# A planner's lock rule for the first layer, and the last squares of a norm summed by TensorE

## The chip, the cores and the metric

The kernel runs on one core of a Trainium2 chip, in one launch. The metric is the time of the whole program on the device in microseconds (us), less is better. The engines are named as the profile names them: PE is TensorE's matmuls and PEld its weight loads, DVE is VectorE, ACT is ScalarE, POOL is GpSimd, and SP is the queue from which most transfers are issued. L536 is line 536 of the kernel.

## The reference

One step of a decoder trunk of two layers, width 1024, over 1024 prompt tokens and 8 x 4 sample tokens, all in float32: 1056 columns in the kernel, which keeps tokens along the free axis.

```python
def _rmsnorm(x, gain):
    xf = x.astype(jnp.float32)
    y = xf * lax.rsqrt(jnp.mean(xf * xf, axis=-1, keepdims=True) + EPS)
    return (y * gain.astype(jnp.float32)).astype(x.dtype)

# _trunk: layer 0, layer 1, final norm
x = x + lru_branch(_rmsnorm(x, g0) @ w_in) @ w_out      # convolution, gates, linear recurrence, SiLU gate
x = x + hgrn_branch(_rmsnorm(x, g1) @ w_in) @ w_out     # gated linear attention with state, SiLU gate
return _rmsnorm(x, final_gain), states
```

The rest of the reference (the convolution, both recurrences, their states) is the same in both kernels and is left out here.

## The kernel before

**Products.** Every product is made of three float32r matmuls per 128 rows of the inner dimension (`mm3`, L245 to L247): the operands are split in a high and a low part, and high x high, high x low and low x high are added up in a bank of PSUM. The 1056 columns of the first layer are worked in three chunks of 352. A weight's high part is a copy on ACT (L387 and others), its low part a subtraction (L332) on DVE or POOL.

**The planner.** Nothing is issued in the order in which it is written. [...] Steps of PE with `main=True` keep their order among themselves; the others are free. `plan` is a list scheduler over the engines, `back` turns a finished plan into new keys, `run` repeats this eight times and takes the best, and for the first layer `search` then tries 3000 random changes of the keys in the first 60 us of the plan. The steps are issued in the order of the best plan, so one changed estimate can move many steps. Each engine serves its queue in order. The lock enters `plan` in two places: a POOL step with `both` sets `held` to its end, and a DVE step with `both` that would start before `held` is taken to wait for it.

```python
            if both and e == "DVE" and held > t0:
                us = max(us, held - t0 + us - 0.13)
            ...
            if both and e == "POOL":
                held = end
```

**The start of the first layer.** Eight blocks of x are loaded for each chunk, and six weights for the first six products (gates and convolution inputs of three tiles). For the first chunk, the unscaled x times the gain is split and multiplied at once; the scale 1/rms of the columns is put on when a product leaves PSUM. So the first chunk's products run ahead of its norm and are held in the four banks `mm`. The norm goes so (`squares`, `norm`): ACT and POOL square the blocks (L439, L437), DVE adds them up (L442), PE sums over the partitions with a column of ones (L281), DVE scales the sums (L454), POOL raises them to -0.5 (L456), DVE spreads them on a diagonal (L457 for 256 columns, L460 for 96), PE makes of it a row for all partitions (L462), and for the first chunk ACT copies that out (L884). DVE then reads the products, times the scale (`evac`: L536 for a gate, L489 for a convolution input). For the second and third chunk the scaled x is split before it is multiplied: L467 scales, ACT's L468 makes the high part, L332 the low part. PE fills the time before its operands are there with 48 small matmuls of ones (L738).

**The end.** The last two heads of the second layer's output product are worked as a loop over three ranges of columns, `OUT` = 424, 376 and 256, and in each over eight rows of 128 features. A row is six matmuls, DVE adds the residual (L1841), ACT squares the result (L1843), and POOL adds the square to the range's accumulator `acc` (L1852). A range's norm is made while the next range runs: at its row `RM` = 3 `summed` puts one matmul for each 128 columns on PE (`norm_sum`, L281) and `roots` makes the scales (L1784 on DVE, L1787 on POOL, then the diagonal L1788 and, for a rest under 128 columns, L1792); at row `SM` = 6 `spread` (L1798) makes the row of scales on PE, and `finish` scales the eight rows (DVE L1818, POOL L1816) and sends them out. Sums and spread are `main` steps. In the last range PE sums each square of rows 4 to 7 itself.

Of the kernel before, what the change touches and what calls it, by code (L numbers as in the profile page):

```python
# [19 lines left out]
ALU = mybir.AluOpType  # L20
# [10 lines left out]
SPOTS, SPOTS0 = (6, 9, 0, 2), (2, 5, -1, -1)  # L31
LAST = "12b675b43", "12b67b453", "12b675b43", "1b267543"
K2 = 8 - K1
RM, SM = 3, 6
OUT = ((0, 424), (424, 376), (800, 256))

D = 1024
SEQ = 1024
# [6 lines left out]
KD = D // 128  # L45
ML = WL // 128
H = 8
EPS = 1e-6
# [3 lines left out]
class Flow:  # L52
# [5 lines left out]
    TURNS = 8  # L58
    ends = []

    def __init__(self, until=None, side=1.2):


        self.until = until
        self.side = side
        self.ops = []
        self.writer = {}
        self.readers = {}
        self.main = None
# [32 lines left out]
    def plan(self, key, stop=None):  # L102

        n = len(self.ops)
        left = [len(o[3]) for o in self.ops]
        ready = [0.0] * n
        wait = {e: [] for e in self.ENGINES}
        free = dict.fromkeys(self.ENGINES, 0.0)
        dma = held = 0.0
        for i in range(n):  # L110
            if not left[i]:
                wait[self.ops[i][0]].append(i)
        starts, ends, took, order = [0.0] * n, [0.0] * n, [0.0] * n, []
        for _ in range(n):
            t0, e = min((max(free[e], min(ready[i] for i in q)), e) for e, q in wait.items() if q)
            q = wait[e]
            i = min((j for j in q if ready[j] <= t0), key=lambda j: (key[j], j))
            q.remove(i)
            order.append(i)
            _, us, _, _, _, kb, _, both = self.ops[i]  # L120
            if both and e == "DVE" and held > t0:
                us = max(us, held - t0 + us - 0.13)
            starts[i] = t0
            free[e] = end = t0 + us
            if both and e == "POOL":
# [88 lines left out]
def tile_trunk(ctx: ExitStack, tc: tile.TileContext, xT, prm, hc, w0, wg, wo0, w1, wo1, s_in,  # L214
               yT, h_out, c_out, sp_out, ss_out):
    nc = tc.nc
    V, S, G, T, Q = nc.vector, nc.scalar, nc.gpsimd, nc.tensor, nc.sync
# [57 lines left out]
    def spans(n):  # L275
        return [(a, min(128, n - a)) for a in range(0, n, 128)]

    def norm_sum(sums, acc, n, start, stop):

        for s, (a, u) in zip(sums, spans(n)):  # L280
            T.matmul(s[:u], acc[:, a:a + u], ones[:, :1], start=start, stop=stop)  # L281
# [18 lines left out]
    with ExitStack() as l0:  # L300
        pl = l0.enter_context(tc.tile_pool(name="l0", bufs=1, reuse_waits="tile"))
        fl = Flow("PE")
# [21 lines left out]
        def dve(n, emit, r, w, prio=5, both=False):  # L324
            fl.add("DVE", 0.13 + 0.0011 * n, emit, r, w, prio, both=both)
# [42 lines left out]
        mm, hg = banks("mm", 4), banks("hg", 4)  # L368
# [567 lines left out]

    with ExitStack() as l1:
        p1 = l1.enter_context(tc.tile_pool(name="l1", bufs=1, reuse_waits="tile"))
        fl = Flow(side=0.4)
        banks8 = [next(mm) for _ in range(4)] + [next(hg) for _ in range(4)]  # L940
        mm, side, hg = cycle(banks8[:NMM]), cycle(banks8[NMM:4]), cycle(banks8[4:])
        chains = banks8[:2], banks8[2:4]
# [830 lines left out]
        accs, sqs, dgs, sb = cycle(spare[:2]), cycle(spare[2:5]), cycle(spare[5:7]), spare[7]  # L1773
        nr2 = cycle([(fixed(f"nr2{i}", [128, 4], F32, p1), ("nr2", i)) for i in range(2)])

        def roots(n, sums, ready):

            r, rk = next(nr2)
            dg, dk = next(dgs)
            f, u = n // 128, n % 128  # L1780
            dve(4, lambda: V.memset(r, 1.0), (), (rk,), 0)
            srcs = [(slice(i, i + 1), s[:w]) for i, (s, (_, w)) in enumerate(zip(sums, spans(n)))]
            for q, src in srcs:
                dve(4, lambda q=q, src=src: V.tensor_scalar(r[:src.shape[0], q], src, 1.0 / D, EPS, op0=ALU.mult, op1=ALU.add),  # L1784
                    ready, (rk,), 0)
            w = len(srcs)
            fl.add("POOL", 0.85, lambda: G.tensor_tensor(r[:, :w], r[:, :w], mhalf[:, :w], op=ALU.pow), (rk,), (rk,), 0)  # L1787
            dve(128 * f, lambda: V.tensor_tensor(dg[:, :128 * f].rearrange("p (i n) -> p i n", i=f),  # L1788
                                                 ident[:, None, :].to_broadcast([128, f, 128]),
                                                 r[:, :f, None].to_broadcast([128, f, 128]), op=ALU.mult), (rk,), (dk,), 0)  # L1790
            if u:
                dve(u, lambda: V.tensor_scalar(dg[:, 128 * f:n], ident[:, :u], r[:, f:f + 1], None, op0=ALU.mult), (rk,), (dk,), 0)  # L1792
            return dg[:, :n], dk

        def spread(n, dg, dk, main):

            bc, bk = next(hg)
            fl.add("PE", 0.002 * n, lambda: T.matmul(bc[:, :n], ones, dg, start=True, stop=True), (dk,), (bk,), 0, main=main)  # L1798
            return bc[:, :n], bk

        def summed(acc, ak, n):
            s, sk = next(hg)
            sums = [s[:, i:i + 1] for i in range(4)]
            fl.add("PE", 0.7, lambda: norm_sum(sums, acc, n, True, True), (ak,), (sk,), 0, main=True)
            return roots(n, sums, (sk,))

        def finish(a, n, bc, bk):
            q = slice(a, a + n)
            own = KD - 3 if a else KD
            if a:  # L1810
                act(n, lambda: S.copy(sb[0][:, :n], bc), (bk,), (sb[1],), 0)
            for k in (*range(own, KD), *range(own)):
                x, xk = x2[k][:, q], ykeys(Y2 + k, a, n)
                if k >= own:
                    act(n, lambda x=x, k=k: S.activation(x, x, AF.Copy, scale=pc("gf", k)), xk, xk, 1)
                    pool(n, lambda x=x: G.tensor_tensor(x, x, sb[0][:, :n], op=ALU.mult), (sb[1], *xk), xk, 1)  # L1816
                else:
                    dve(n, lambda x=x, k=k: V.scalar_tensor_tensor(x, x, pc("gf", k), bc, op0=ALU.mult, op1=ALU.mult), (bk, *xk), xk, 1)  # L1818
                dma(yT[k][:, q], x, xk, (), 1, n / 2, S if k % 2 else Q)

        for a, n in OUT:
            q = slice(a, a + n)
            final = a + n == TOK
            cs = [c for c in range(NCH) if c * CH < a + n and (c + 1) * CH > a]
            acc, ak = next(accs)
            for m in range(KD):
                if a and m == RM:
                    dg = summed(*prev[:2], prev[3])
                if a and m == SM:
                    finish(*prev[2:], *spread(prev[3], *dg, True))  # L1830
# [12 lines left out]
                act(n, lambda sq=sq, x=x, n=n: S.activation(sq[:, :n], x, AF.Square), xk, (sk,), 1)  # L1843
                if final and m >= 4:
                    if m == 4:
                        sums = [(next(hg)) for _ in spans(n)]
                        sumk = [k for _, k in sums]
                        sums = [s[:, :1] for s, _ in sums]
                        fl.add("PE", 0.3, lambda acc=acc, n=n, sums=sums: norm_sum(sums, acc, n, True, False), (ak,), sumk, 0)
                    fl.add("PE", 0.3, lambda sq=sq, n=n, m=m, sums=sums: norm_sum(sums, sq, n, False, m == KD - 1), (sk, *sumk), sumk, 0)  # L1850
                elif m:
                    pool(n, lambda acc=acc, sq=sq, n=n: G.tensor_tensor(acc[:, :n], acc[:, :n], sq[:, :n], op=ALU.add), (sk, ak), (ak,), 1)  # L1852
            prev = acc, ak, a, n
# [76 lines left out]
```

## Time and profile before

| what | us |
|---|---|
| median of three runs | 1077.92 (1074.05 to 1078.39) |
| profiled execution | 1074.69 |
| its span, first to last instruction | 1072.9 |
| PE busy | 1046.7 (98%) |
| DVE busy | 783.4 (73%) |
| ACT busy | 675.9 (63%) |
| POOL busy | 510.3 (48%) |
| mean granted clock of TensorE | 0.991 |

The first layer runs to about 520 us, the second from there, and the loop of the final norm from 1031.7 us. A row of the timeline gives start, duration, engine, line, operation, the tiles written and read, their shapes and how many instructions are merged; what stands in brackets is how long the engine was idle before it and for whom it waited. A row of the waits gives who waited for whom, the sum, the number of times, and the longest.

### The profile page before, as it was taken

How to read it: one execution, taken by the hardware profiler on the slowest of the kernel's cores; microseconds unless marked ns; L12 is line 12 of the kernel's file. 1: busy time of each engine (PE TensorE's matmuls, PEld its weight loads, DVE VectorE, ACT ScalarE, POOL GpSimd, SP SyncE). 2: the span in 40 equal slices, each digit the busy share in tenths (PEclk: the TensorE clock that was granted, in tenths of full speed). 3: DMA queues.
4: the chain of work that ended last, by engine and by line, in shares of the span. 5: the costliest groups of instructions: out<-in, count | busy, mean ns of one | idle time of the engine just before them, and what ended most of it. 6: DMA issues, size and time to landing. Idle time of an engine off the chain costs nothing.

```text
span 1072.9 us, 25911 instructions
## 1 busy us (share of the span) xinstructions
PE 1046.7 (98%) x10092; PEld 1018.4 (95%) x10092; DVE 783.4 (73%) x1536; ACT 675.9 (63%) x1526; POOL 510.3 (48%) x532
## 2 busy tenths in 40 slices
PE   9899999999999999999988999999999999999996
PEld 9899999999999999999988999999999989989995
DVE  7899997689798689256678565756557576899646
ACT  6559665966765776233377585858676755765443
POOL 3326443354535355644544555545455453434465
PEclk9899999999999999999999999999999999999998
DMA  8202122123662586444595565656576662734544
GB/s 283 75 15 58 36 64 61 50 64 93 200 201 68 155 260 198 143 155 167 178 226 123 115 163 109 166 103 163 113 177 143 143 156 66 247 109 118 118 96 162
DMA packets 90331, 143.24 MB, mean 134 GB/s; under 512 B 11104, under 2 KB 55904, under 8 KB 90208
## 3 DMA queue, kind: packets, MB, share of 16 engines
q1 hardware_dynamic: 74656, 112.46, 33.5%
q0 software_dynamic: 13248, 26.35, 14.7%
q10 hardware_dynamic: 2304, 2.77, 0.8%
q8 instruction: 79, 1.29, 0.5%
q14 instruction: 44, 0.36, 0.1%
HBM read 81.60 MB, written 33.05 MB: 107 GB/s over the span
## 4 chain that ended last, share of the span: by engine, by line
PE 86%; DVE 8%; DMA 3%; ACT 1%; issue 1%; POOL 0%; ACTq 0%; POOLq 0%; DVEq 0%; SPq 0%
PE mm L245 24%; PE mm L247 23%; PE mm L246 23%; PE hg L1060 2%; PE hg L1277 1%; PE hg L576 1%; PE hg L1169 1%; PE hg L1279 1%; PE hg L1223 1%; PE hg L245 1%; PE hg L247 1%; PE hg L246 1%; DVE t L332 1%; DMA wraw<-in_w_dram 1%; DMA a<-xn 1%; DVE sg L1042 1%
## 5 line engine op out<-in xcount | busy, mean ns | idle before, releaser
L245 PE MATMUL mm<-xh,whi 128*128 128x352 f32 (+1 forms) x1147 | 355.1, 310 | 5.1 <-ACT os L1247 2.8
L246 PE MATMUL mm<-xl,whi 128*128 128x352 f32 (+1 forms) x1147 | 349.9, 305 | 0.2 <-DVE xl L877 0.2
L247 PE MATMUL mm<-xh,wlo 128*128 128x352 f32 (+1 forms) x1147 | 350.0, 305 | 0.0
L245 PEld LDWEIGHTS mm<-xh,whi 128*128 128x128 f32 x1147 | 216.3, 189 | 8.4 <-ACT os L1247 3.0
L246 PEld LDWEIGHTS mm<-xl,whi 128*128 128x128 f32 x1147 | 216.7, 189 | 2.3 <-DVE xl L877 0.4
L247 PEld LDWEIGHTS mm<-xh,wlo 128*128 128x128 f32 x1147 | 216.5, 189 | 0.0
L332 POOL TENSOR_TENSOR wlo<-wraw,whi 128x512 fp32r<-128x512 f32 (+1 forms) x66 | 94.8, 1444 | 88.1 <-ACT whi L387 71.2
L247 PE MATMUL mm<-t,wlo 128*128 128x264 f32 x408 | 115.9, 284 | 2.9 <-DMA wlo<-wraw 2.8
L245 PE MATMUL mm<-t,whi 128*128 128x264 f32 x408 | 118.1, 289 | 0.0
L246 PE MATMUL mm<-t,whi 128*128 128x264 f32 x408 | 115.8, 284 | 0.0
L508 DVE SCALAR_TENSOR_TENSOR k<-xb,prm_sb,k 128x352 f32<-128x352 f32 (+2 forms) x144 | 88.6, 628 | 13.0 <-ACT k L505 9.9
L247 PEld LDWEIGHTS mm<-t,wlo 128*128 128x128 f32 x408 | 76.6, 188 | 3.3 <-DMA wlo<-wraw 3.3
L245 PEld LDWEIGHTS mm<-t,whi 128*128 128x128 f32 x408 | 76.9, 188 | 0.3
L246 PEld LDWEIGHTS mm<-t,whi 128*128 128x128 f32 x408 | 76.9, 189 | 0.1
L591 POOL TENSOR_TENSOR k<-X 128x352 f32<-128x352 f32 x36 | 45.2, 1262 | 55.5 <-DVE R L592 42.8
L1539 DVE TENSOR_TENSOR k<-mm,k 128x264 f32<-128x264 f32 x72 | 30.6, 429 | 53.9 <-PE mm L247 51.5
L319 POOL DMA_DIRECT2D wlo<-wraw x51 | 44.6, 886 | 52.6 <-ACT wlo L318 32.5
L245 PE MATMUL mm<-yh,whi 128*128 128x352 f32 x153 | 49.9, 326 | 0.0
L246 PE MATMUL mm<-yl,whi 128*128 128x352 f32 x153 | 49.4, 323 | 0.0
L247 PE MATMUL mm<-yh,wlo 128*128 128x352 f32 x153 | 49.4, 323 | 0.0
L319 POOL DMA_DIRECT2D wlo<-R x30 | 28.0, 935 | 40.7 <-ACT wlo L318 38.2
L387 ACT CAST whi<-wraw 128x512 fp32r<-128x512 f32 (+1 forms) x63 | 36.1, 591 | 16.8 <-DMA wraw<-in_w_dram 7.2
(423 smaller groups left out, 2723.2 us busy)
## 6 DMA issues: line engine op xcount, KB each, us to landing
wraw<-in_w_dram SPq DMA_DIRECT2D x88, 256.0 KB, 3.2
wlo<-wraw POOLq DMA_DIRECT2D x51, 256.0 KB, 4.1
wlo<-R POOLq DMA_DIRECT2D x30, 256.0 KB, 4.2
wraw<-in_wo_dram SPq DMA_DIRECT2D x37, 192.0 KB, 2.7
ysum<-sg SPq DMA_DIRECT2D x9, 528.0 KB, 4.2
si<-in_s_in_dram SPq DMA_DIRECT2D x8, 512.0 KB, 4.2
R<-in_w_dram SPq DMA_DIRECT2D x16, 256.0 KB, 3.7
out_ss_out_dram<-si SPq DMA_DIRECT2D x8, 512.0 KB, 2.7
```

Source lines behind the costliest of these rows:

```text
L245: T.matmul(out, wh, xh, start=first, stop=False, skip_group_check=chained)
L246: T.matmul(out, wh, xl, start=False, stop=False, skip_group_check=chained)
L247: T.matmul(out, wl, xh, start=False, stop=last, skip_group_check=chained)
L319: fl.add("POOL", 0.93, lambda: G.dma_start(dst.bitcast(F32), src, accum_op=ALU.add), (*r, *w), w, prio, n / 2)
L332: emit = lambda: e.tensor_tensor(b, x, a.bitcast(F32), op=ALU.subtract)
L387: act(m, lambda hi=hi, raw=raw, m=m: S.copy(hi[:, :m], raw[:, :m]), rk, (hk,), prio)
L508: dve(u, lambda src=src, dst=dst, sh=sh, k=k: V.scalar_tensor_tensor(dst, sh(src, k), pc("cw", 12 * k + m), dst, op0=ALU.mult, op1=ALU.add ...
L576: fl.add("PE", 0.62, lambda ps=ps, i=i, c=c: T.matmul(ps[:96, :CH], gs[:, i, :], ST[:96, chunk(c)], start=True, stop=True), (("gs",), *((" ...
L591: pool(CH, lambda x=x, a=a, b=b: G.tensor_tensor(x, a.bitcast(F32), b.bitcast(F32), op=ALU.add), (ak, bk), (xk,), 3)
L1042: dve(n // 2, lambda sv=sv, dv=dv, s=s, f=f: V.tensor_tensor(dv[:, :, s, :], sv[:, :, s, :], f, op=ALU.mult), (*sk, *gk), dk if i == o els ...
L1060: T.matmul(ps[32 * j:32 * j + 32, n * w:n * w + w], B[:, o:o + 32], q(slice(o, o + 32)), start=True, stop=True, tile_position=(0, 32 * j))
L1539: dve(QT, lambda: V.tensor_tensor(o[0], z[0], u[0], op=ALU.add), (z[1], u[1]), (o[1],), 0)
```

## The change

There are two parts.

The planner gets a switch `issues`. [...] It is on for the first layer, whose POOL steps without the mark are the power steps of the norms and the iotas of the masks; the second layer keeps the old rule.

In the final norm, for the first two ranges, POOL adds up the squares of rows 0 to 5 only. PE sums three things into three sets of four columns of one PSUM bank: the accumulator, row 6's square and row 7's square (`PS` = 6). `roots` gets `groups` = 3 and lets DVE reduce the three sets (new lines 1788 and 1790: one `tensor_reduce` for the full blocks of 128 columns, one for a rest, then one scaling). These sums are no longer `main` steps, so the planner places them. The ranges become 416, 384 and 256.

```diff
-OUT = ((0, 424), (424, 376), (800, 256))
+RM, SM, FM, PS = 3, 6, 3, 6
+OUT = ((0, 416), (416, 384), (800, 256))
...
-    def __init__(self, until=None, side=1.2):
+    def __init__(self, until=None, side=1.2, issues=True):
...
-            if both and e == "POOL":
+            if e == "POOL" and (both or self.issues):
                 held = end
...
-        fl = Flow(side=0.4)
+        fl = Flow(side=0.4, issues=False)
...
-        def roots(n, sums, ready):
+        def roots(n, sums, ready, groups=1):
...
+            if groups > 1:
+                view = sums.rearrange("p (g i) -> p i g", i=4)
+                for t in ([128, 0, f],) + (([u, f, f + 1],) if u else ()):
+                    dve(4, lambda t=t: V.tensor_reduce(r[:t[0], t[1]:t[2]], view[:t[0], t[1]:t[2]], op=ALU.add, axis=mybir.AxisListType.X),
+                        ready, (rk,), 0)
+                dve(4, lambda: V.tensor_scalar(r[:, :w], r[:, :w], 1.0 / D, EPS, op0=ALU.mult, op1=ALU.add), (rk,), (rk,), 0)
...
-        def summed(acc, ak, n):
-            s, sk = next(hg)
-            sums = [s[:, i:i + 1] for i in range(4)]
-            fl.add("PE", 0.7, lambda: norm_sum(sums, acc, n, True, True), (ak,), (sk,), 0, main=True)
-            return roots(n, sums, (sk,))
...
                 if a and m == RM:
-                    dg = summed(*prev[:2], prev[3])
+                    dg = roots(prev[1], prev[2], prev[3], KD - PS + 1)
...
+                elif m >= PS and not final:
+                    if m == PS:
+                        s_, sk_ = next(hg)
+                        fl.add("PE", 0.5, lambda s_=s_, acc=acc, n=n: norm_sum([s_[:, i:i + 1] for i in range(4)], acc, n, True, True), (ak,), (sk_,), 0)
+                    o = 4 * (m - PS + 1)
+                    fl.add("PE", 0.5, lambda s_=s_, sq=sq, n=n, o=o: norm_sum([s_[:, o + i:o + i + 1] for i in range(4)], sq, n, True, True), (sk,), (sk_,), 0)
                 elif m:
                     pool(n, lambda acc=acc, sq=sq, n=n: G.tensor_tensor(acc[:, :n], acc[:, :n], sq[:, :n], op=ALU.add), (sk, ak), (ak,), 1)
```

In the second layer the queues stay as they were up to the final norm. In the first layer every queue is rearranged, most in the first 60 us. The lines of the changed kernel are numbered one higher there (L443 is the old L442), and up to line 1776.

The first place is PE's queue in the fourth product of the start (its operands are `xh`, `xl`, `yh` and `yl`), at the spread of the first chunk's norm. Before:

```order
L247 MATMUL mm<-xh,yl_153 128x352
L245 MATMUL mm<-xh,yh_150 128x352
L246 MATMUL mm<-xl,yh_150 128x352
L247 MATMUL mm<-xh,yl_153 128x352
L462 MATMUL hg<-k,ones 128x352
```

Now, at the same spread:

```order
L246 MATMUL mm<-xh,yh_150 128x352
L247 MATMUL mm<-xl,yh_150 128x352
L248 MATMUL mm<-xh,yl_153 128x352
L282 MATMUL hg<-ones,R 128x1 x2
L282 MATMUL hg<-ones,R 96x1
L463 MATMUL hg<-k,ones 128x352
```

Before, the spread stands behind the 15th matmul of the product and the sums of the second chunk's norm behind the 3rd; now both stand together behind the 6th.

The second place is DVE's queue from the end of the first chunk's diagonal to the first read of a product (`R` and `xo` are the accumulator and the squares of the second and third chunk, `nr` the scales, `smalls` small constants of the layer, `mm` the products). Before:

```order
L460 TENSOR_SCALAR k<-ident,nr_130 128x96
L442 TENSOR_TENSOR R<-R,xo_135 128x352
L442 TENSOR_TENSOR R<-R,xo_136 128x352
L454 TENSOR_SCALAR nr_131<-hg 128x2
L454 TENSOR_SCALAR nr_131<-hg 96x1
L442 TENSOR_TENSOR R<-R,xo_137 128x352
L442 TENSOR_TENSOR R<-R,xo_135 128x352
L750 TENSOR_TENSOR smalls<-smalls 128x12
L750 TENSOR_SCALAR smalls<-smalls 128x12
L442 TENSOR_TENSOR R<-R,xo_136 128x352
L442 TENSOR_TENSOR R<-R,xo_137 128x352
L536 TENSOR_TENSOR sg<-mm,R 128x352
```

Now:

```order
L461 TENSOR_SCALAR k<-ident,nr_130 128x96
L443 TENSOR_TENSOR R<-R,xo_137 128x352
L443 TENSOR_TENSOR R<-R,xo_135 128x352
L443 TENSOR_TENSOR R<-R,xo_136 128x352
L751 TENSOR_SCALAR smalls<-smalls 128x12
L751 TENSOR_TENSOR smalls<-smalls 128x12
L455 TENSOR_SCALAR nr_131<-hg 128x2
L455 TENSOR_SCALAR nr_131<-hg 96x1
L443 TENSOR_TENSOR R<-R,xo_137 128x352
L443 TENSOR_TENSOR R<-R,xo_135 128x352
L450 MEMSET nr_130 128x4
L537 TENSOR_TENSOR sg<-mm,R 128x352 x3
```

Five additions stand there instead of six, and three products are read one behind the other, the third bank first. Ahead of these rows, from the first instruction on, DVE's queue holds 14 such additions where it held 15, and seven small steps on `smalls` with 12 elements besides the reciprocal where it held ten. Two additions of the third chunk now come some 30 instructions later.

The third place is PE's queue in the final norm, at the sums of the first range inside the second (`t` holds weights; `R`, `sg` and `a` hold the accumulator and the squares). Before:

```order
L247 MATMUL mm<-xh,t_5231 128x376
L281 MATMUL hg<-ones,R 128x1 x3
L281 MATMUL hg<-ones,R 40x1
L245 MATMUL mm<-xh,t_5232 128x376
L246 MATMUL mm<-xl,t_5232 128x376
```

Now:

```order
L248 MATMUL mm<-xh,t_5230 128x384
L282 MATMUL hg<-ones,R 128x1 x3
L282 MATMUL hg<-ones,R 32x1
L282 MATMUL hg<-ones,sg 128x1 x3
L282 MATMUL hg<-ones,sg 32x1
L282 MATMUL hg<-ones,a 128x1 x3
L282 MATMUL hg<-ones,a 32x1
L246 MATMUL mm<-xh,t_5231 128x384
```

Twelve sums stand where four stood, and one row of features earlier (behind row 1 of the second range instead of row 2). For the second range it is nine instead of three, again one row earlier. The spreads stay ahead of row 6.

More of the change, by code (lines that the diff above doesn't have):

```diff
@@ L33 @@
 K2 = 8 - K1
-RM, SM = 3, 6
-OUT = ((0, 424), (424, 376), (800, 256))
+RM, SM, FM, PS = 3, 6, 3, 6
+OUT = ((0, 416), (416, 384), (800, 256))
 D = 1024
@@ L59 @@
     ends = []
-    def __init__(self, until=None, side=1.2):
+    def __init__(self, until=None, side=1.2, issues=True):
         self.until = until
         self.side = side
+        self.issues = issues
         self.ops = []
@@ L1781, in roots @@
             dve(4, lambda: V.memset(r, 1.0), (), (rk,), 0)
[L1782 to L1785, printed above, removed]
+            srcs = [(slice(i, i + 1), s[:w]) for i, (s, (_, w)) in enumerate(zip(sums, spans(n)))] if groups == 1 else spans(n)
             w = len(srcs)
+            if groups > 1:
[4 more added lines that the diff above has]
+                dve(4, lambda: V.tensor_scalar(r[:, :w], r[:, :w], 1.0 / D, EPS, op0=ALU.mult, op1=ALU.add), (rk,), (rk,), 0)
+            else:
+                for q, src in srcs:
+                    dve(4, lambda q=q, src=src: V.tensor_scalar(r[:src.shape[0], q], src, 1.0 / D, EPS, op0=ALU.mult, op1=ALU.add),
+                        ready, (rk,), 0)
             fl.add("POOL", 0.85, lambda: G.tensor_tensor(r[:, :w], r[:, :w], mhalf[:, :w], op=ALU.pow), (rk,), (rk,), 0)
@@ L1799, in spread @@
             return bc[:, :n], bk
-        def summed(acc, ak, n):
-            s, sk = next(hg)
-            sums = [s[:, i:i + 1] for i in range(4)]
-            fl.add("PE", 0.7, lambda: norm_sum(sums, acc, n, True, True), (ak,), (sk,), 0, main=True)
-            return roots(n, sums, (sk,))
         def finish(a, n, bc, bk):
             q = slice(a, a + n)
-            own = KD - 3 if a else KD
+            own = KD - FM if a else KD
             if a:
@@ L1827, in tile_trunk @@
                 if a and m == RM:
-                    dg = summed(*prev[:2], prev[3])
+                    dg = roots(prev[1], prev[2], prev[3], KD - PS + 1)
                 if a and m == SM:
-                    finish(*prev[2:], *spread(prev[3], *dg, True))
+                    finish(*prev[:2], *spread(prev[1], *dg, True))
                 ps, pk = next(mm)
@@ L1850, in tile_trunk @@
                     fl.add("PE", 0.3, lambda sq=sq, n=n, m=m, sums=sums: norm_sum(sums, sq, n, False, m == KD - 1), (sk, *sumk), sumk, 0)
+                elif m >= PS and not final:
[4 more added lines that the diff above has]
+                    fl.add("PE", 0.5, lambda s_=s_, sq=sq, n=n, o=o: norm_sum([s_[:, o + i:o + i + 1] for i in range(4)], sq, n, True, True), (sk,), (sk_,), 0)
                 elif m:
                     pool(n, lambda acc=acc, sq=sq, n=n: G.tensor_tensor(acc[:, :n], acc[:, :n], sq[:, :n], op=ALU.add), (sk, ak), (ak,), 1)
-            prev = acc, ak, a, n
+            prev = a, n, s_[:, :4 * (KD - PS + 1)], (sk_,)
         spin, wk = next(mm)
```

## The prediction

> **What bounds the kernel now.** I read the page's busy shares first, then TensorE's waits in three stretches, then the busy time by stretch with the granted clock, and last the timeline around the two places that the change reaches.
>
> ```profile
> PE 1046.7 (98%) x10092; PEld 1018.4 (95%) x10092; DVE 783.4 (73%) x1536; ACT 675.9 (63%) x1526; POOL 510.3 (48%) x532
> ```
>
> TensorE (PE) is busy for 98% of the span. What an edit can win lies in its few waits, in its clock, and in work that is taken from it.
>
> ```profile
> PE mm L245 <- DVE sg L536: 3.8, 1, 3.8
> ```
>
> This row, of PE's waits up to 480 us, is the only long one of the first layer: the fifth product of the start finds all four banks of PSUM full, because VectorE (DVE) has not yet read the first (L536). The waits in the final norm stand with Part 2. The busy time by stretch (columns: stretch, length, PE, PEld, DVE, ACT, POOL busy with counts, granted clock, DMA share, GB/s) says what a wait costs besides itself:
>
> ```profile
> 36.40:48.58 12.18, 12.18 (x56) 11.68 (x57) 10.35 (x24) 6.78 (x14) 2.54 (x5) 0.72 0.27 81
> ...
> 100.00:500.00 400.00, 400.00 (x2456) 394.72 (x2455) 306.37 (x504) 251.08 (x488) 190.60 (x205) 1.00 0.42 127
> 540.00:560.00 20.00, 17.17 (x249) 16.48 (x247) 15.89 (x21) 14.67 (x28) 10.09 (x9) 1.00 0.93 213
> 880.00:900.00 20.00, 17.22 (x138) 16.35 (x138) 15.42 (x27) 6.11 (x17) 9.48 (x9) 0.91 0.14 43
> ```
>
> Behind the wait of 3.8 us the granted clock is 0.72 for 12.18 us: 0.28 x 12.18 = 3.4 us are lost there. So the start costs 3.8 + 3.4 = 7.2 us. Of two stretches in the second layer where PE idles 2.8 us (20 - 17.2), one shows a lower clock (0.91, so 0.09 x 20 = 1.8 us), one does not. From 100 to 500 us PE is never idle.
>
> [...]
>
> **Part 1: the first layer's order.** [...]
>
> ```profile
> 23.66 1.08 DVE L442 TENSOR_TENSOR R<-R,xo 128x352 f32<-128x352 f32 x2
> ...
> 31.45 1.16 DVE L442 TENSOR_TENSOR R<-R,xo 128x352 f32<-128x352 f32 x2
> 31.56 1.14 POOL L456 TENSOR_TENSOR nr<-nr,mhalf 128x3 f32<-128x3 f32 x1 [1.34 <-DVE nr L454]
> ```
>
> Two additions take 1.08 us alone and 1.16 us beside a power step. So I expect nothing of the rule itself and read the new order as another draw of the search. [...]
>
> What the draw changes is the way to the first L536. In the trace it runs so (PE, then DVE, POOL and ACT):
>
> ```profile
> 30.37 0.83 PE L462 MATMUL hg<-k,ones 128*128 128x352 f32 x2
> ...
> 32.32 0.32 PE L247 MATMUL mm<-xh,yl 128*128 128x352 f32 x1
> 36.40 0.43 PE L245 MATMUL mm<-xh,yh 128*128 128x352 f32 x1 [3.76 <-DVE sg L536]
> ...
> 43.69 0.41 PE L245 MATMUL mm<-xh,yh 128*128 128x352 f32 x1
> ...
> 48.58 0.32 PE L245 MATMUL mm<-xh,X 128*128 128x352 f32 x1
> ```
> ```profile
> 28.96 1.32 DVE L460 TENSOR_SCALAR k<-ident,nr 128x96 f32<-128x96 f32 x1
> ...
> 32.52 0.16 DVE L750 TENSOR_TENSOR smalls<-smalls 128x12 f32<-128x12 f32 x1
> 32.72 1.26 DVE L750 TENSOR_SCALAR smalls<-smalls 128x12 f32<-128x12 f32 x1
> 33.90 2.01 DVE L442 TENSOR_TENSOR R<-R,xo 128x352 f32<-128x352 f32 x2
> 35.84 0.51 DVE L536 TENSOR_TENSOR sg<-mm,R 128x352 f32<-128x352 f32 x1
> ```
> ```profile
> 32.66 1.29 POOL L332 TENSOR_TENSOR yl<-wraw,yh 128x512 fp32r<-128x512 f32 x1
> 33.89 1.64 POOL L554 TENSOR_TENSOR gl<-wraw,gh 128x512 fp32r<-128x512 f32 x1
> ```
> ```profile
> 32.69 0.43 ACT L884 COPY R<-hg 128x352 f32<-128x352 f32 x1
> ```
>
> The scales of the first 352 columns go from L460 (done 30.28) over PE's spread L462 and ACT's copy L884 (done 33.12) to L536. The copy was ready 2.7 us before L536 began: what held it was DVE's own queue, six additions L442, two small steps (and two tiny ones of the next norm, L454), in all 35.84 - 30.28 = 5.56 us. In it a small step of 0.16 us took 1.26 and a pair of 1.08 took 2.01, both beside big POOL subtractions (L332, L554): 1.1 + 0.9 = 2.0 us of holding. Six additions of 1.08 / 2, two small steps of 0.16 and the holding make up the 5.56.
>
> In the new order, up to L460 DVE has one addition (1.08 / 2 = 0.54) and three small steps (3 x 0.16 = 0.48) fewer: L460 is done 1.0 us sooner, at 29.3, if the loads land alike (up to the last block of the first columns SP and ACT have issued the same blocks, only in another sequence). Bounds: 28 (a holding of 1.1 fewer) and 31 (one more, and a late load). Behind L460 come five additions (5 x 0.54 = 2.7), two small steps (0.3) and two evacuations, since now the third bank is read before the first (2 x 0.5 = 1.0). One subtraction (L332) still falls in, L554 comes behind: holding of 1.1. Sum 5.1, so the first bank is free at 34.4; without the holding at 33.3. ACT's copy, needed by then, now stands ahead of ACT's last two squares and has from 30.1 (29.3 + 0.83, the spread) on to be done: time enough.
>
> PE: it ends the fourth product at 32.32 + 0.32 = 32.64 as before. The sums and the spread in its queue only move: the spread from behind the 15th matmul of that product to behind the 6th, 9 x 0.163 = 1.5 us sooner at 28.9 (0.163 is (48.58 - 43.69) / 30 matmuls). With L460 at 29.3 that spread waits 0.4 us or so, and everything behind it: PE is at 33.0. So 3.76 us of waiting become 0.4 + 1.4 = 1.8 or, without the holding, 0.7; I take 1.3, saved 2.5, in pieces too short for the clock to fall by the rows above: saved 3.4 more. Together 5.9.
>
> What is late next are the second columns' operands:
>
> ```profile
> 47.40 0.95 DVE L332 TENSOR_TENSOR xl<-sg,xh 128x352 fp32r<-128x352 f32 x2
> ```
>
> They were finished at 48.35, and the product that uses them began at 48.58 and needed the last of them about 6 x 3 x 0.163 = 2.9 us later: 3 us of slack. PE comes there 5.9 us sooner; DVE's chain to them starts at the second spread, which moves with L460 and the evacuations by some 2 to 4 us. So 0 to 2 us return as waits; I take 0.9. Other local swaps go on to 500 us, where PE's queue stays full: 0 expected, at worst another wait like the one of 3.8. Layer 1's queues are the same up to the final norm, so it just starts earlier. Part 1: -2.5 - 3.4 + 0.9 = -5.0 us, bounds -7.2 (all of it goes) and +3.8 - 1.0 = +2.8 (another such wait, and only L460's 1.0 us won).
>
> **Part 2: the final norm.** For the first two ranges POOL no longer adds the squares of rows 6 and 7 (off PE's path, except for the last addition), and PE sums three sets: 12 sums in place of 4, and 9 in place of 3.
>
> ```profile
> 1044.03 0.89 PE L281 MATMUL hg<-ones,R 128*128 128x1 f32 x8
> ...
> 1044.85 0.44 PE L245 MATMUL mm<-xh,t 128*128 128x376 f32 x1
> ...
> 1048.76 0.98 PE L1798 MATMUL hg<-sg,ones 128*128 128x424 f32 x2 [0.55 <-DVE sg L1792]
> ...
> 1054.42 0.81 PE L281 MATMUL hg<-ones,R 128*128 128x1 f32 x6 [0.45 <-POOL R L1852]
> ...
> 1058.56 0.90 PE L1798 MATMUL hg<-sg,ones 128*128 128x376 f32 x2 [1.11 <-DVE sg L1792]
> ```
> ```profile
> 1044.96 0.35 DVE L1784 TENSOR_SCALAR nr<-hg 128x1 f32<-128x1 f32 x4 [0.18 <-PE hg L281]
> ```
>
> Four sums hold PE for 1044.85 - 1044.03 = 0.82 us, 0.205 each; 14 more cost 2.9 us, all on the path. What they buy: the sums stand one row earlier (behind row 1 instead of 2) and wait for no addition (0.45), the chain to the first spread has four rows instead of three to hide in (0.55 goes), and the one to the second spread likewise, but only in part. There DVE's queue holds the diagonal (now one piece of 384, L1788) behind the evacuation of row 3; I keep 0.5 of its 1.11. The two reductions and the one scaling that replace four or three scalings have no row; the nearest are those scalings, L1784, four in 0.35 us. Two reductions and a scaling are taken as 0.1 to 0.6 us, so at most 0.3 more, and they are covered by the added row; without that cover 0.3 more at each spread, which lies inside the bounds. The new ranges move 8 columns from the first to the second: nothing. Behind the second spread all is as before. Part 2: +2.9 - 0.45 - 0.55 - 0.6 = +1.3, less the slow restarts after three waits (0.44 above against 0.32 in the first layer's rows, 0.1 each): +1.0. Bounds: +0.2 (all of 1.11 goes, restarts too) and +2.9 (no wait goes).
>
> **Sum.** -5.0 + 1.0 = -4.0 us. The profiled execution took 1074.69 us (span 1072.9), so 1070.7 in its terms; it lies 3.2 below the median of the runs, 1077.92, and near the fastest, 1074.05. Against the median: 1073.9.
>
> **The rivals.** (a) The start is wholly covered: POOL's subtraction falls elsewhere, L536 is ready with PE, both 3.8 and 3.4 go, and the slack at the second columns covers what follows: -7.2, and +1.0 at the end, so -6.2 and 1071.7. For it: without the holding the rest above is only 0.7 us. Against it: 5.1 us of DVE work stand between L460 and the evacuation, and PE has 18 matmuls, 2.9 us, to do meanwhile.
> (b) The rest of the wait is 2.8 us or more and the clock falls again: then -1 or -2 at the start, +1 at the end: 1077.4. For it: the row at 880 us, and a load that lands 1 us late is enough.
> (c) Slower: PE's queue is served in order, and the spread now stands nine matmuls earlier. The fifth product cannot start before L460 + 0.83 for the spread + 18 x 0.163 = 2.9 us; for 36.40 us as now L460 may be as late as 32.7, and each microsecond beyond is a loss. At 35 us it costs 2.3 us, the clock falls as before, a further wait like the 2.8 us ones follows at the second columns, and the norm's +1.0 joins: +6.1, 1084. Against it: the queue up to L460 is shorter than before.
> (d) The order changes and the time does not, because the start's gain returns as waits for the second columns (2 instead of 0.9, and a clock that falls there for 3.4): -4.0 + 1.1 + 3.4 = +0.5, 1078.4. That the change doesn't move anything is ruled out by the order of instructions.
>
> **How the numbers follow.** Forecast (-2 to -6 us) 0.45; (a) 0.18; (b) 0.13; (c) 0.15, since one late load or one longer holding ahead of L460 is enough to reach it; (d) 0.09. The range from 1069.5 to 1080 holds the forecast, (a), (b), (d) and the runs' own spread, and leaves (c) and the tails out. Half a per cent, 5.4 us, is about what a measurement of this kernel can tell from no change. Faster by more: most of (a), 0.16, and a fifth of the forecast, 0.09: 0.25. Slower by more: (c), 0.15. Within: 0.60.
>
> **What would show it.** Right: no wait of PE above 2 us before 60 us, granted clock 1.00 there, the first product of the second columns (X weights) at about 43.5 instead of 48.58 us; in the norm 24 and 18 records of sums where there were 8 and 6, spreads waiting at most 0.5 us, and POOL without additions for rows 6 and 7. Wrong: a wait of 2.8 us or more at L462 or L245 before 45 us, a clock below 1 behind it, new PE waits between 45 and 500 us, or spreads of the norm that still wait 1 us.

## The result, and the profile after

The changed kernel takes 1069.46 us (median of six runs, 1068.03 to 1074.35), the kernel before, beside it, 1077.43 (six runs, 1074.05 to 1078.42). The ratio is 0.9937 with an interval of 0.9913 to 0.9961: 6.8 us less, between 4.2 and 9.4. The forecast was 4.0 us less and 1073.9 us; the measured median lies at the lower edge of its range (1069.5 to 1080.0), 0.04 us below that figure, while before ran 0.5 us faster here than the median that the forecast was set against. The direction and the mechanism at the start were right. The size was 2.8 us short, and it is nearer to rival (a), 6.2 us less, than to the forecast. That the total came so near was partly luck: as shown below, the first layer gave 3.7 us more than forecast and the norm took 1.9 more. The profiled execution took 1068.75 us with a span of 1067.0, where before showed 1074.69 and 1072.9.

Lines of the changed kernel are one higher than before's (L537 is the old L536); in the final norm L1806 is the spread and L1820 the scaling. TensorE's waits up to 480 us, and the busy time over the same stretch as the row with a clock of 0.72 in the prediction:

```profile
PE mm L246 <- DVE sg L537: 0.6, 1, 0.6
```
```profile
36.40:48.58 12.18, 12.09 (x76) 11.80 (x75) 12.14 (x25) 6.49 (x14) 2.22 (x3) 1.00 0.12 37
```

The wait of 3.8 us is 0.6, and behind it the clock is 1.00 instead of 0.72: 76 matmuls fit where 56 did. The timeline of the start, TensorE first, then VectorE from the diagonal to the first reads of a product:

```profile
28.17 0.84 PE L463 MATMUL hg<-k,ones 128*128 128x352 f32 x2
...
31.58 0.32 PE L248 MATMUL mm<-xh,yl 128*128 128x352 f32 x1
32.50 0.43 PE L246 MATMUL mm<-xh,yh 128*128 128x352 f32 x1 [0.59 <-DVE sg L537]
...
40.97 0.32 PE L246 MATMUL mm<-xh,X 128*128 128x352 f32 x1
```
```profile
27.22 0.26 DVE L461 TENSOR_SCALAR k<-ident,nr 128x96 f32<-128x96 f32 x1
27.40 2.69 DVE L443 TENSOR_TENSOR R<-R,xo 128x352 f32<-128x352 f32 x3
...
30.42 1.14 DVE L443 TENSOR_TENSOR R<-R,xo 128x352 f32<-128x352 f32 x2
31.49 0.52 DVE L537 TENSOR_TENSOR sg<-mm,R 128x352 f32<-128x352 f32 x1
```

The diagonal (L461) is done at 27.48, 2.8 us sooner than the 30.28 of before; one piece of it took 0.26 us where it took 1.32. The first product of the second columns starts at 40.97 instead of 48.58: 7.6 us sooner.

At the end, the sums and spreads of the first two ranges and the matmuls behind the first sums:

```profile
1034.17 0.88 PE L282 MATMUL hg<-ones,R 128*128 128x1 f32 x8
1034.98 0.98 PE L282 MATMUL hg<-ones,sg 128*128 128x1 f32 x8
1035.89 0.98 PE L282 MATMUL hg<-ones,a 128*128 128x1 f32 x8
1036.80 0.45 PE L246 MATMUL mm<-xh,t 128*128 128x384 f32 x1
...
1038.31 0.52 PE L246 MATMUL mm<-xh,t 128*128 128x384 f32 x1
1038.63 0.52 PE L247 MATMUL mm<-xl,t 128*128 128x384 f32 x1
...
1042.66 0.86 PE L1806 MATMUL hg<-sg,ones 128*128 128x416 f32 x2
1046.87 0.73 PE L282 MATMUL hg<-ones,R 128*128 128x1 f32 x6
1047.46 1.48 PE L282 MATMUL hg<-ones,a 128*128 128x1 f32 x12
1048.80 0.36 PE L246 MATMUL mm<-xh,t 128*128 128x256 f32 x1
...
1052.57 0.91 PE L1806 MATMUL hg<-sg,ones 128*128 128x384 f32 x2 [0.73 <-DVE sg L1820]
```

Twelve sums took 2.63 us (1034.17 to 1036.80), nine 1.93, and the first spread no longer waits. But a new loss stands behind the first sums: the matmuls at 1038 follow each other at 0.32 us instead of 0.17. The busy time in two stretches shows why; each is 3.41 us long, and the granted clock is the number before the last two:

```profile
1034.12:1037.54 3.42, 3.42 (x30) 3.33 (x29) 0.95 (x4) 0.84 (x2) 1.13 (x2) 1.00 0.00 0
1037.54:1040.95 3.41, 3.41 (x13) 3.41 (x12) 1.51 (x4) 0.53 (x1) 1.91 (x2) 0.50 0.00 0
```

The stretch that holds the sums is followed by one at half clock, which costs half of 3.41: 1.7 us. Set against before by common instructions, the changed kernel is 8.7 us ahead at 507 us, still 8.7 ahead when the loop of the norm begins, and 5.8 ahead at the last spread (1059.12 against 1064.96). In this pair of traces the first layer gave 8.7 us and the norm took 2.9.

The clock records of the traces of before and of the change hold only 1.0 and 0.5. So the span of every timed execution can be divided in two: what was lost to the half clock, (1 - mean clock) x span, and the rest. Means over the executions (clock to 0.001, so about 0.5 us for a single one; the half clock after the last product, from 1064.45 us on in the trace of before and from 1058.02 in that of the change, which slows only the last spread, is in it):

| kernel | executions | span | lost to clock | rest |
|---|---|---|---|---|
| before (beside the variants) | 54 | 1074.7 | 11.0 | 1063.7 |
| the change | 6 | 1068.3 | 9.1 | 1059.2 |
| order alone | 6 | 1066.0 | 7.3 | 1058.7 |
| norm alone | 12 | 1077.1 | 12.3 | 1064.8 |
| sums apart | 4 | 1066.8 | 6.9 | 1059.9 |
| one row's squares | 5 | 1065.8 | 4.9 | 1060.9 |
| before, wait filled | 7 | 1070.4 | 5.5 | 1064.9 |

### The profile page after: what moved, and what is told of

It reads as the page before. It is cut to its first block, busy times and chain, and to the rows that moved or that the text cites. A ratio compares the mean times of both kernels' runs of the same rounds, so it can differ in the third digit from the quotient of the medians.

```text
span 1067.0 us, 25951 instructions
## 1 busy us (share of the span) xinstructions
PE 1046.7 (98%) x10120; PEld 1019.2 (96%) x10120; DVE 782.0 (73%) x1533; ACT 676.2 (63%) x1526; POOL 505.5 (47%) x528
## 4 chain that ended last, share of the span: by engine, by line
PE 88%; DVE 7%; DMA 2%; ACT 1%; issue 1%; POOL 0%; POOLq 0%; ACTq 0%; SPq 0%; DVEq 0%
PE mm L246 24%; PE mm L248 24%; PE mm L247 24%; PE hg L1061 2%; PE hg L1278 1%; PE hg L577 1%; PE hg L1170 1%; PE hg L1280 1%; PE hg L1224 1%; PE hg L246 1%; PE hg L247 1%; PE hg L248 1%; DVE sg L1043 1%; DMA wlo<-wraw 1%; PE hg L1322 1%
```

## The experiments

**The order alone, and the norm alone.** The first is the kernel before with the rule's switch, the second the change without it:

```diff
 e1_order: before, with
-            if both and e == "POOL":
+            if e == "POOL" and (both or self.issues):
 e2_norm: the change, with
-    def __init__(self, until=None, side=1.2, issues=True):
+    def __init__(self, until=None, side=1.2, issues=False):
```

> Only the first layer's order of the change; the final norm (and the ranges 424, 376, 256) as before. Theory A, the start is the gain: no wait of TensorE over 1 us and no lowered clock before 60 us, the first product of the second columns some 7.5 us sooner than the 48.58 us of before, and no half clock behind the four sums of the norm: 7.5 to 8.5 us less than before, 2.5 to 3 us less than the change (about 1069 against 1077.4). Rival B, part of the gain came from the pace of TensorE in that one profiled execution (1.2 us between 175 and 500 us): then 6 to 7 us less than before. Rival C, the clock behind the wait of before was low by chance of that execution: then only the wait goes, 3.5 to 4.5 us less.

> Only the final norm of the change (three sets of sums, ranges 416, 384, 256); the first layer's order as before. Theory A: the wait of 3.8 us and the clock of about 0.72 behind it are there as before, the norm costs 1.4 us by its sums less waits, and 1.6 us more in executions in which the clock is halved behind the twelve sums: 1.4 to 3.0 us slower than before (1079 to 1080.5). Rival B: the sums alone cost 2.9 us and the waits give nothing back, the clock stays: +2.9. Rival C, the norm wins by itself as its waits go: 0 to 1 us faster.

Measured: the order alone 1066.82 us, ratio 0.9918 (0.9896 to 0.9940), against 1076.81 for before beside it; the norm alone 1079.21, ratio 1.0021 (1.0005 to 1.0037). In the table -8.7 and +2.4 us of span come to -6.3, against -6.4 for the whole change: nothing shows that the parts act on each other. Waits of the order alone, up to 480 us and in the norm's loop (up to 1056 us):

```profile
PE mm L246 <- DVE sg L537: 1.1, 1, 1.1
...
PE hg L1799 <- DVE sg L1793: 1.5, 2, 1.0
PE hg L282 <- POOL R L1853: 0.8, 1, 0.8
```

and of the norm alone the wait and the stretch at the start:

```profile
PE mm L246 <- DVE sg L537: 4.1, 1, 4.1
```
```profile
36.40:48.58 12.18, 12.18 (x59) 11.68 (x58) 10.57 (x23) 6.38 (x14) 3.13 (x5) 0.72 0.27 89
```

Theory A holds for both, but for a wait of 1.1 us in the order alone where at most 1 was expected: the whole gain is the order's, the norm costs. Rival C of the order is out, since the clock fell behind the wait in each trace with the old order and seed 1. The 6 to 7 us of rival B touch the interval (6.5 to 11.2 us less); its reason, a pace that belongs to one execution, is answered below under the pace of the matmuls. The norm costs 1.1 us in the rest and 1.3 in the clock, in the means. Not every execution pays the second: in the trace of the norm alone the twelve sums (1042.73 to 1045.36) lay across the end of a stretch of 3.41 us (1043.82), and the clock stayed full.

**Where the norm's clock goes.** Two variants of the change: the sums apart (the accumulator's four in front of row 1 of the next range, the squares' eight where they were), and only the last row summed by TensorE.

```diff
 e3_apart
+                for at_, ks_, f_ in [p for p in pend if p[0] == m] if a else ():
+                    fl.add("PE", 0.5, f_, ks_, (prev[3][0],), 0, main=True)
 e4_one_row
-RM, SM, FM, PS = 3, 6, 3, 6
+RM, SM, FM, PS = 3, 6, 3, 7
```

> The change with the same 21 sums, but those of the accumulator stand one row of features earlier than those of the two squares: runs of 4 and 8 sums (0.8 and 1.8 us) instead of one run of 12 (2.6 us) in the first range, 3 and 6 in the second. Theory A (a run of tiny matmuls of 2.6 us counts as idle for the clock): no half clock behind the sums, the first range 1.6 us shorter, 1.0 to 1.6 us less than the change where that lowers its clock in most executions. Rival B (the loss of clock there has another cause, for instance the time since the last event): the clock still falls between the sums and the spread, same time as the change within 0.5 us.

> The change with only the last row's squares summed by TensorE (two sets: 8 and 6 sums instead of 12 and 9); VectorE's neighbour GpSimd adds row 6 again, and the sums stand one row later in the first range. Theory A: 7 sums fewer at 0.205 us are 1.4 us less, no half clock behind a run of 1.7 us is 1.6 us less, the spreads wait 0.3 to 0.6 us more: 1.5 to 2.7 us less than the change. Rival B (no clock effect): 0.8 to 1.1 us less. Rival C: the sums wait for GpSimd's addition of row 6 again (0.45 us each) and the spreads for 0.5 and 1.1 us as before: the same as the change within 0.5 us.

Measured: 1068.51 (ratio 0.9927, 0.9908 to 0.9945) and 1066.87 (0.9917, 0.9900 to 0.9935). In the trace of the sums apart the clock is full over the sums and behind them:

```profile
1034.52:1038.20 3.68, 3.68 (x32) 3.59 (x31) 1.12 (x2) 1.43 (x3) 0.27 (x1) 1.00 0.00 0
1038.20:1042.00 3.80, 3.80 (x24) 3.80 (x23) 2.59 (x6) 1.05 (x2) 2.83 (x4) 1.00 0.00 0
```

The traces are as theory A has them, and the time lost to the clock falls from 9.1 to 6.9 and 4.9 us. Not all of that is the norm's: the order alone, which has no more than four sums in a row in the first two ranges, loses 7.3. Between these kernels and the change, too, the intervals overlap: about 1 and 2.6 us less is likely and not shown by the times alone. With one row's squares the spreads wait more than forecast, which takes back the seven sums:

```profile
PE hg L1806 <- DVE sg L1800: 1.6, 1, 1.6
PE hg L1806 <- DVE sg L1796: 0.8, 1, 0.8
```

**Tiny matmuls by themselves.** Runs of 4, 12 and 20 one-column matmuls, put into the first layer, where TensorE never waits:

```diff
+                    for i in range(tiny):
+                        T.matmul(ps[:, i:i + 1], ones, ones[:, :1], start=True, stop=True)
```

> The change with 36 runs of extra one-column matmuls of ones put in front of every third product of the first layer, whose results are overwritten at once: in turn 4, 12 and 20 of them (0.8, 2.5 and 4.1 us). It measures the price of such runs by itself. Theory A (they count as idle for the clock, in windows of 3.4 us): none of the runs of 4 is followed by a half clock, about a third to a half of the runs of 12 and nearly all of the runs of 20; each half clock costs 1.7 us, so that the whole takes 432 x 0.205 = 89 us and some 25 to 30 us of lost clock more. Rival B (they count as work): clock 1.00 throughout, 89 us more and no further loss.

Measured: 1193.71 us (one run). Each run of 4 held TensorE for 0.81 us, of 12 for 2.60, of 20 for 4.4 or more. A half clock began during the run or within 3.5 us behind it for 0 of 12, 4 of 12 and 12 of 12. Of the 124 us more than the change, 31 are lost clock (40.5 against 9.1). One run of 20, and the clock in the two stretches around its end:

```profile
313.02 4.52 PE L412 MATMUL mm<-ones 128*128 128x1 f32 x40
...
318.62 0.49 PE L248 MATMUL mm<-yh,wlo 128*128 128x352 f32 x1
```
```profile
314.47:317.88 3.41, 3.41 (x31) 3.41 (x31) 0.00 (x0) 2.35 (x2) 0.00 (x0) 1.00 0.47 147
317.88:321.29 3.41, 3.41 (x12) 2.83 (x11) 1.26 (x3) 0.08 (x1) 0.22 (x1) 0.50 0.00 0
```

Theory A, in count and in size: the profile shows TensorE busy for the whole first stretch (3.41 of 3.41 us), and the clock in the next is 0.50 all the same. The operand of ones is not the reason: in the changed kernel products of ones with 128 columns (L739) are TensorE's only work up to 10.23 us, and the clock is full from 6.71 us (1.00 from 6.71 to 10.23).

**The wait without its idleness.** The kernel before, with ten small products of ones inside the wait of 3.8 us:

```diff
+                    for _ in range(fill if ks[-1] == n - 1 else 0):
+                        T.matmul(ps[:, CH:CH + 128], ones, ones, start=True, stop=True)
```

> The kernel before, with ten small products of ones (128 x 128, results unused) in TensorE's queue between the fourth and the fifth product of the start, that is inside the wait of 3.8 us; every other queue as before. Theory A (the clock falls because TensorE idles there): the first read of the bank comes when it came, the fifth product starts at 36.4 us as before, the clock stays at 1.00 behind it, and 3.4 us are saved: about 1073. Rival B (the clock behind the wait falls for another reason): clock 0.72 as before, same time as before within 0.5 us. Rival C (small products do not count as work): the same as B. Were the small products longer than the wait, they would cost their excess.

Measured: 1070.67 us (seven runs, 1068.83 to 1077.38), ratio 0.9942 (0.9918 to 0.9966). The rest of the span is 1.2 us above before's (0.3 above the twelve executions beside it), the lost clock 5.5 instead of 11.0 us. So, in the means, the clock behind the wait is a cost of its own that work of no use removes; rivals B and C, no gain, are out. The gain is more than the 3.4 forecast, and why is open: no trace shows a start in which the filling sufficed. The one trace is of the slowest execution, in which the filling ended too soon (35.04 us, the fifth product began at 36.87) and the clock fell all the same:

```profile
34.35:37.76 3.41, 1.58 (x12) 1.39 (x11) 3.31 (x7) 0.79 (x2) 1.06 (x2) 1.00 0.31 85
37.76:44.59 6.83, 6.83 (x26) 6.33 (x25) 5.21 (x13) 3.49 (x7) 0.83 (x2) 0.50 0.42 136
```

**The rule or the draw.** The search for the first layer's order with other seeds, by the old rule and by the new, in which every GpSimd step sets `held` (final norm as before in all):

```diff
-        rng = Random(1)
+        rng = Random(2)        # e5, e7; Random(3) in e6, e8
```

> The kernel before with another seed of the search for the first layer's order (2 instead of 1); old lock rule. Theory A, a draw: the new rule says nothing true of the chip, and each search ends with another start; the wait for the first evacuation comes out anywhere from 0.5 to 5 us, and with it the clock: time between 1066 and 1079. Theory B, the rule: plans made with the old rule all run into a wait of 3 us or more at the start, because the plan overlooks what GpSimd's power step does to VectorE: 1075 to 1079.

> As the run with seed 2 and the old rule, with seed 3. Theory A: between 1066 and 1079, not near the other old-rule run but by chance. Theory B: 1075 to 1079.

> The first layer's order made with the new rule and seed 2, the norm as before. Theory A: between 1066 and 1079, with a wait of 0.5 to 5 us for the first evacuation. Theory B, the rule: a wait under 1.5 us there, the clock not lowered before 60 us, 1066 to 1069 like the run with seed 1.

> As the run with seed 2 and the new rule, with seed 3. Theory A: between 1066 and 1079. Theory B: 1066 to 1069, no wait over 1.5 us before 60 us.

| rule, seed | long waits of TensorE before 60 us | half clock there | median | ratio |
|---|---|---|---|---|
| old, 1 (before) | 3.8 | 6.8 us | 1075.62 (1076.81 beside new, 1) | 1 |
| old, 2 | 0.8 + 0.4 | none | 1071.49 | 0.9955 (0.9943 to 0.9968) |
| old, 3 | 3.3 + 1.3 | 6.8 us | 1074.73 | 0.9994 (0.9977 to 1.0010) |
| new, 1 (order alone) | 1.1 | none | 1066.82 | 0.9918 (0.9896 to 0.9940) |
| new, 2 | 0.8 + 0.7 + 0.7 | none | 1072.63 | 0.9956 (0.9934 to 0.9977) |
| new, 3 | 1.0 + 1.3 | none | 1070.55 | 0.9955 (0.9936 to 0.9975) |

Theory B fails on both sides: a plan by the old rule avoids the wait (seed 2), and plans by the new rule come out at 1070.6 and 1072.6, not at 1066 to 1069. All six lie where theory A had them, in a range wide enough for almost any outcome. The waits and clocks of the table are those of one execution each; for the new rule with seed 2 it is the fastest of ten (1066.41 us). Nor do the power steps here and in the prediction show the lock that the rule assumes. In the changed kernel a pair of additions takes 1.14 us beside the power step, as a pair does in before at 30.20 us with GpSimd idle from 30.22; VectorE's L443 at 30.42 above runs through it and L537 follows at once; GpSimd's row is

```profile
30.58 1.08 POOL L457 TENSOR_TENSOR nr<-nr,mhalf 128x3 f32<-128x3 f32 x1 [1.51 <-DVE nr L455]
```

Still, two of three plans by the old rule ran into a wait over 3 us and none of three by the new. Three against three does not settle whether the rule makes better plans on average.

**The pace of the matmuls.** Between 60 and 500 us consecutive matmuls of 352 columns into `mm` follow each other at 160.93 ns on average in before and at 160.08 in the change. Before was run once more, and in a variant of the change each third product got one small matmul ahead of it:

```diff
 e12_shifted
+                    T.matmul(ps[:, :32], xs[0][0][:, :128], xs[0][0][:, :32], start=True, stop=True)
```

> The kernel before once more, for a second trace. Theory A: the same wait of about 3.8 us and a half clock of 6.8 us behind it, at the same windows counted from the first full clock. Of the pace between 175 and 500 us, which was 161.1 ns a matmul of 352 columns in the first trace against 159.0 in stretches of the changed kernel's: if it belongs to the execution, it comes out anywhere between these; if to the kernel's order, 161 again.

> The change with one small float32r matmul of 32 columns (result overwritten) in front of every third product of the first layer, 36 in all: each moves TensorE's later instructions by one matmul and its weight load. It asks where the pace of the 352-column matmuls between 60 and 500 us comes from, which was 160.9 ns in every trace with the old order and 160.1 ns in every trace with the new one (2340 matmuls, 2.0 us). Theory A, the position of TensorE's instructions sets it: in the stretches that ran at 159.2 ns (128 to 175 and 298 to 325 us of the change) some products go at 161 ns and some at 159, changing at the added matmuls. Theory B, it is not the position: these stretches stay at 159.2 ns between the added matmuls, and the whole takes 36 x 0.1 to 0.2 us, 4 to 7 us, more than the change.

Matmuls begun between 100 and 500 us, in this order: before, before again, the change, order alone, new rule with seed 2:

```profile
100.00:500.00 400.00, 400.00 (x2456) 394.72 (x2455) 306.37 (x504) 251.08 (x488) 190.60 (x205) 1.00 0.42 127
100.00:500.00 400.00, 400.00 (x2456) 394.72 (x2455) 307.85 (x504) 250.48 (x488) 189.25 (x205) 1.00 0.42 127
100.00:500.00 400.00, 400.00 (x2467) 394.50 (x2467) 307.95 (x511) 249.49 (x484) 185.77 (x202) 1.00 0.42 128
100.00:500.00 400.00, 400.00 (x2467) 394.50 (x2466) 307.94 (x511) 249.12 (x484) 184.96 (x200) 1.00 0.42 128
100.00:500.00 400.00, 400.00 (x2456) 394.52 (x2455) 307.93 (x507) 247.80 (x480) 188.81 (x207) 1.00 0.41 126
```

Before again took 1075.54 us, with a wait of 4.0 us and the same 6.8 us of half clock. The pace belongs to the kernel and not to the execution: 160.93 ns in each of four traces of kernels with the first layer as before, 160.08 in each of four with it as in the change, 160.8 to 161.1 with the other seeds. Over 2340 matmuls 0.85 ns are 2.0 us; set against before by common instructions, each of the four gains 1.4 us between 130 and 500 us, and the rest was not traced. The shifted variant (1071.69 us, one run) went at 160.4: the stretch that ran at 159.2 ns now ran at 160.3, with later products at 159 and 160.4 in turn. That is neither of the two forecasts. The pace answers to the added matmuls, but by which property is open.

## Why the prediction was right, and where it was short

**The start: the mechanism right, its terms too small.** The forecast had L460 done at 29.3; it was done at 27.48, below its bound of 28. It counted one addition and three small steps less (1.0 us); the piece of the diagonal itself, held to 1.32 us before and 0.26 now, is 1.06 more, and the remaining 0.7 was not traced. From there to the second evacuation, which TensorE needed, it took 4.9 us (27.48 to 32.4); the forecast had 5.1, with its 1.1 of holding (the three additions at 27.40 took 2.69 us where three took 3 x 0.54). So the wait fell by 3.2 us where 2.5 stood in the sum, and the rival "wholly covered" describes the start better than the forecast does. TensorE also ended the fourth product at 31.90 us, where the forecast kept before's 32.64 and added 0.4 for the spread. That is 0.7 us more, of which a part can be the execution's: in four traces with the old start that end lies up to 0.9 us apart. The clock term stood at 3.4 and is 3.7 in the means of the order alone. Of the 0.9 us that were to come back at the second columns, about 0.35 did, 0.25 of it where one matmul followed 0.41 instead of 0.16 us behind the one before it.

**What the sum lacked.** The pace. The forecast let the queue run as fast as before from 100 to 500 us, and no row of before shows that it could go faster. By common instructions the changed kernel is 0.7 us ahead at the end of the fourth product, 3.9 behind the wait, 7.6 at the second columns, 7.3 at 55 us and, with the pace, 8.7 at 500 us, where the forecast had 5.0.

**The end: the waits right, a clock term missing.** The 21 sums cost 3.06 us more than the seven (2.63 + 1.93 against 0.82 + 0.68; forecast 2.9). The waits of 0.45 and 0.55 went. Of 1.11 at the second spread 0.38 went, where 0.6 was expected, and what is left is no wait for the diagonal any more. VectorE's rows there:

```profile
1051.01 0.95 DVE L1796 TENSOR_TENSOR sg<-ident,nr 128x384 f32<-128x384 f32 x1
1051.88 0.63 DVE L1820 SCALAR_TENSOR_TENSOR sg<-sg,prm_sb,hg 128x416 f32<-128x416 f32 x1
```

The diagonal (L1796) was done at 1051.96, the spread began at 1052.57, right behind a scaling of the first range (L1820, to 1052.51) that the profile names as its releaser. That scaling reads the first range's row of scales from `hg`; with four banks in turn the second spread is given the same bank, so it waits for the last reader. In the means over twelve executions of the norm alone, the part of the span outside the half clock grew by 1.1 us, about the 1.0 forecast. Missing was the half clock behind twelve sums, 1.3 us in the means and 1.7 in the traced execution: the forecast priced the sums by the 0.205 us that each holds TensorE and gave them no clock term. (The part's lower bound, +0.2, is +0.5 by its own terms, 2.9 - 0.45 - 0.55 - 1.11 - 0.3; the result lies above both.)

**The rule as such** was expected to be worth nothing. The power steps of the traces agree with it; the six plans do not settle it. The pair above took 1.14 us beside the power step, and its second addition ended inside the power step's row (31.56 against 31.66): this three-column step did not hold it.

**The rivals.** The slower one needed L460 after 32.7 and got 27.48. "The clock still falls" and "the gain returns at the second columns" are both out: clock 1.00, 0.35 us returned.

## What to carry to other kernels

Short waits of TensorE are to be priced with the clock that follows them; here that was 3.4 us behind a wait of 3.8 and nothing behind one of 0.6. Runs of one-column matmuls cost clock here too (a half clock with none of 12 runs of 0.81 us, 4 of 12 of 2.60 us and 12 of 12 of 4.4 us or more), so many small sums in a row are better spread between products or left to another engine: the order alone (1066.82) and the variant with one row's squares (1066.87) both have lower medians than the change, though by less than the intervals can tell apart, and intervals wholly below before. A searched order is a draw: before a new planning rule is believed, several seeds by each rule should be run.

## What the runs showed of the hardware that was not expected

In the traces of before and of the change each half clock up to the last product lasted 3.41 us or twice that (before: 37.03 to 43.86 and 886.95 to 890.37; the change: 546.02 to 549.43 and 1037.54 to 1040.95) and began a whole number of such stretches behind the first full clock (9 and 258; 158 and 302). That point lay 6.31 us behind the first instruction in before and 6.71 in the change, so the stretches lie differently in the two. In the stretches ahead of these four half clocks TensorE was without work for 2.78, 2.01, 3.09 and 2.47 us, one-column matmuls counted as no work. The 2.8 us that the prediction read from the row at 880 us were spread over 20 us; in the stretch ahead of that half clock (883.54 to 886.95) they were 2.0. In the row at 540 us, where the clock stayed full, no such stretch had more than 1.8 of its 2.8 us (552.45 to 555.86).

The other surprise is the pace: the same matmuls in the same sequence, with TensorE never waiting and the clock full, took 159 or 161 ns, though the order alone with seed 1 and the new rule with seeds 2 and 3 have TensorE's queue alike from about 85 us on, and the other engines' queues from about 160 us on. Between 188 and 228 us the change, whose first layer is that of the order alone, runs at 159.1 ns all the same, and the new rule with seed 3 at 161.1.
